# Input normalising on ScalarE and VectorE shared anew, and the low-rank weights' scaling moved to ScalarE, in the first stage of a hybrid encoder

## The chip, the core and the metric
The kernel runs on one core of one Trainium2 chip. The core has a matrix engine (TensorE, PE in the profile; its weight loads are PEld), a vector engine (VectorE, DVE), a scalar engine (ScalarE, ACT), a third elementwise engine (GpSimd, POOL), and a sync engine (SP) that mostly issues DMAs. Each engine takes its own instructions in a fixed order and waits on semaphores for the others. The metric is the time of one launch in microseconds, as the median of several runs.

## The reference
One layer of a post-norm encoder, batch 1, 1024 positions, width 1024, in float32. The input is normalised, projected to 2048 columns, given to four kinds of mixers, projected back, normalised, put through a SwiGLU block and normalised again:

```python
h = _layer_norm(x, ln0_g, ln0_b)
p = h @ w_in[l]
p_ssm, p_rkv, p_conv, p_fft = jnp.split(p, splits, axis=-1)
y_a = _s5_mixer(p_ssm, ...)          # diagonal complex state space, two directions
y_b = _rwkv7_mixer(h, p_rkv, ...)    # delta-rule state update, two directions
y_c = _short_conv_mixer(p_conv, conv_w[l])
y_d = _fourier_mixer(p_fft)
y = jnp.concatenate([y_a, y_b, y_c, y_d], axis=-1)
h = _layer_norm(DEEPNORM_ALPHA * h + y @ w_out[l], ln1_g[l], ln1_b[l])
f = (jax.nn.silu(h @ ffn_w1[l]) * (h @ ffn_w3[l])) @ ffn_w2[l]
h = _layer_norm(DEEPNORM_ALPHA * h + f, ln2_g[l], ln2_b[l])
```

The change touches the first norm and, in the RWKV mixer, the low-rank weights. That mixer blends each position of `h` with its neighbour, channel by channel, before it multiplies by a narrow matrix:

```python
dx = jnp.stack([x_prev, x_next]) - xn
xw = xn + dx * mu_w[:, None, None, :]
xa = xn + dx * mu_a[:, None, None, :]
xg = xn + (0.5 * (x_prev + x_next) - xn) * mu_g
```

Since the blend is linear, the kernel multiplies `h` by `(1 - mu) * w` and by `mu * w`, and adds the second product shifted by one position.

## The kernel before, in words
**Accuracy and tiling.** A float32 matmul is done as three matmuls on rounded parts (`mm3`, L159 to L162): high weights by high input (L160), high weights by low input (L161), low weights by high input (L162). So each operand exists twice: the high part is the value rounded to the matmul's format, the low part is what the rounding left. The input after the norm is kept transposed, channels on the partitions, as `HA` (high) and `HB` (low). The weights of a column block of 128 come in as `wraw`, a cast on ACT gives `wh` (L393), a subtraction on POOL gives `wl` (L394). Blocks 2 and 3 of the first stage go into a larger tile, `wfar`, instead. A column block is 96 matmuls over 256 positions each (four quarters of the positions, eight blocks of channels, three products).

**The norm.** `norm0` goes over eight tiles of 128 positions. Per tile: statistics (`row_stats`, on DVE with a square root on ACT at L183), the normalised tile `xn` (L316, DVE, in place of `xt`), then in two halves of four channel blocks: four transposes on PE into `n0ps` (L322), four evacuations with gain and bias into `hf` (ACT at L332, or DVE at L329), a cast to `HA` (L333, DVE) and a subtraction to `HB` (L334, POOL).

**The stages.** `start` weaves the norm with the first four column blocks, two for S5 and two for the Fourier mixer (384 matmuls). Then `build` weaves two strands. The chain, at high priority, is S5 (its tables `s5w`, then products named `s5tp`, `s5k`, `s5pv`, `s5py`), then the RWKV preparation with the first direction's block inverse (`pre`, `pa` fed by `abd`, `pm` fed by `dmn`), then the scan of 32 steps (`px`, `pt`, `pz`, `po`). The other strand, `beside`, holds the rest of the projection: low-rank weights for two directions and the gate (`lora_project`), the RWKV columns, the convolution, Fourier; and then the second direction's inverse, which the scan needs from its step 17 on, and the first parts of the output projection.

**What sets the order.** The code of both strands is given to a scheduler with priorities; it places instructions on each engine by a modelled time. Both strands are issued only after the three instructions in `norm_end`, one each on DVE, ACT and POOL, so these decide where the norm's work ends on each engine and where the other begins. In the kernel before, DVE's of the three is the last `xn`, so S5's DVE work may start while the norm's casts are still going.

**Low-rank weights.** `weights` in `lora_project` loads a narrow matrix as `lraw`, and L903 multiplies it by `mu` per channel into `lmw` on DVE, eight or sixteen small instructions. `lmw` then goes through cast and subtraction like other weights; POOL subtracts `lmw` from `lraw` (L918, L930, L936), which leaves `(1 - mu) * w`, and that goes through the same. L919 adds the two products into `la`.

## Time and profile before
| | |
|---|---|
| median of 3 runs | 1463.02 us (1460.07 to 1464.85) |
| profiled execution | 1465.01 us |
| its span, first to last instruction | 1462.2 us |
| PE busy | 1323.2 us, 90% |
| DVE busy | 1100.0 us, 75% |
| ACT busy | 621.7 us, 43% |
| POOL busy | 575.7 us, 39% |

The span is 2.8 us shorter than the time of the execution it belongs to; what lies around it no instruction shows. Busy shares are averages over stages of very different kinds, so rows of single stages are needed to say what an engine waits for. A wait is put down to the instruction that released it, with the waiting instruction in front of the arrow.

### The profile page before, as it was taken

What the parts mean: (1) busy time and instruction counts of PE and PEld (TensorE: products, weight loads), DVE (VectorE), ACT (ScalarE), POOL (GpSimd) and SP (SyncE); (2) the same over time, 40 slices, a digit from 0 to 9 for tenths busy, and PEclk for the clock granted to TensorE, in tenths of its full rate; (3) what the DMA queues carried; (4) which work ended last, traced back from release to release, by engine and by line L of the source; (5) the groups of instructions that cost most, each with busy time, mean ns of one, the idle gap of its engine ahead of it and who ended that gap; (6) DMA issues with size and microseconds to landing.
All of it is one profiled execution on the core that took longest, in us unless ns stands there. A gap on an engine that the chain in (4) does not pass through costs nothing.

```text
span 1462.2 us, 23749 instructions
## 1 busy us (share of the span) xinstructions
PE 1323.2 (90%) x9072; PEld 1196.4 (82%) x9072; DVE 1100.0 (75%) x1910; ACT 621.7 (43%) x1205; POOL 575.7 (39%) x524
## 2 busy tenths in 40 slices
PE   6968797977797999999877899999999999999997
PEld 5968787766796787877766899999999999888885
DVE  8997966487997685779999866666676665346888
ACT  4312141656324785761426544444444444332231
POOL 6466663153574332325567633333333331000006
PEclk9989998999899898999999899999999999999999
DMA  6111033122325004244312434444444438996752
GB/s 241 49 54 29 13 94 87 44 70 89 87 73 180 2 15 148 84 128 154 118 70 87 138 123 159 147 147 143 157 147 142 150 137 291 385 315 234 273 188 115
DMA packets 97056, 193.95 MB, mean 133 GB/s; under 512 B 24624, under 2 KB 50864, under 8 KB 96944
## 3 DMA queue, kind: packets, MB, share of 16 engines
q1 hardware_dynamic: 94912, 187.59, 38.3%
q10 hardware_dynamic: 2032, 4.86, 1.0%
q8 instruction: 71, 1.16, 0.3%
q14 instruction: 41, 0.34, 0.1%
HBM read 127.41 MB, written 63.96 MB: 131 GB/s over the span
## 4 chain that ended last, share of the span: by engine, by line
PE 42%; DVE 12%; DMA 3%; issue 2%; ACT 1%; POOL 1%; DVEq 0%; SPq 0%; ACTq 0%; POOLq 0%
PE fx L160 5%; PE fx L162 5%; PE fx L161 5%; PE f L160 4%; PE f L162 4%; PE f L161 4%; PE fy L162 2%; PE fy L160 2%; PE fy L161 2%; DVE acc L1435 1%; PE fz L160 1%; PE fz L161 1%; PE fz L162 1%; DMA fw<-w 1%; PE ops L161 1%
## 5 line engine op out<-in xcount | busy, mean ns | idle before, releaser
L160 PE MATMUL proj<-HA,wh 128*128 128x256 f32 x672 | 195.5, 291 | 14.6 <-DVE la L919 11.8
L160 PE MATMUL fx<-H,fc 128*128 128x256 f32 x704 | 196.9, 284 | 5.7 <-ACT fc L1384 2.2
L161 PE MATMUL proj<-HB,wh 128*128 128x256 f32 x672 | 200.1, 298 | 1.7 <-POOL HB L334 1.7
L162 PE MATMUL proj<-HA,wl 128*128 128x256 f32 x672 | 196.6, 293 | 4.1 <-POOL wl L394 4.1
L162 PE MATMUL fx<-H,fc 128*128 128x256 f32 x704 | 197.8, 282 | 2.6 <-DVE fc L1385 2.6
L1385 POOL TENSOR_TENSOR fc<-fw,fc 128x512 fp32r<-128x512 f32 x96 | 137.3, 1432 | 158.5 <-ACT fc L1384 157.7
L161 PE MATMUL fx<-H,fc 128*128 128x256 f32 x704 | 198.5, 282 | 0.0
L160 PEld LDWEIGHTS proj<-HA,wh 128*128 128x128 f32 x672 | 131.8, 196 | 18.4 <-issue 7.7
L162 PEld LDWEIGHTS proj<-HA,wl 128*128 128x128 f32 x672 | 131.5, 196 | 10.0 <-issue 5.5
L160 PEld LDWEIGHTS fx<-H,fc 128*128 128x128 f32 x704 | 132.5, 190 | 7.8 <-ACT fe L1633 2.7
L161 PEld LDWEIGHTS proj<-HB,wh 128*128 128x128 f32 x672 | 131.5, 196 | 7.0 <-issue 4.8
L162 PEld LDWEIGHTS fx<-H,fc 128*128 128x128 f32 x704 | 133.7, 191 | 2.8 <-DVE fc L1385 2.8
L161 PEld LDWEIGHTS fx<-H,fc 128*128 128x128 f32 x704 | 134.1, 191 | 0.1
L160 PE MATMUL f<-fb,fa 128*128 128x512 f32 x276 | 108.9, 395 | 0.0
L162 PE MATMUL f<-fb,fa 128*128 128x512 f32 x276 | 108.9, 394 | 0.0
L161 PE MATMUL f<-fb,fa 128*128 128x512 f32 x276 | 108.7, 394 | 0.0
L160 PE MATMUL fy<-H,fc 128*128 128x256 f32 x352 | 100.0, 284 | 4.7 <-ACT fe L1642 3.6
L162 PE MATMUL fy<-H,fc 128*128 128x256 f32 x352 | 99.5, 284 | 0.2 <-DVE fc L1385 0.2
L161 PE MATMUL fy<-H,fc 128*128 128x256 f32 x352 | 99.5, 283 | 0.0
L1821 POOL TENSOR_TENSOR acc<-acc,g 128x1024 f32<-128x1024 f32 x4 | 11.6, 2904 | 205.8 <-ACT acc L1820 205.8
L1384 ACT CAST fc<-fw 128x512 fp32r<-128x512 f32 x120 | 73.7, 619 | 31.8 <-POOL fc L1385 15.7
L1385 POOL TENSOR_TENSOR fc<-fs,fc 128x512 fp32r<-128x512 f32 x24 | 33.4, 1391 | 119.4 <-ACT fc L1384 116.0
(602 smaller groups left out, 3761.6 us busy)
## 6 DMA issues: line engine op xcount, KB each, us to landing
fa<-d_f SPq DMA_DIRECT2D x77, 512.0 KB, 3.8
d_f<-fg SPq DMA_DIRECT2D x70, 512.0 KB, 2.9
fw<-w SPq DMA_DIRECT2D x48, 512.0 KB, 3.6
fg<-w SPq DMA_DIRECT2D x44, 256.0 KB, 5.3
wraw<-w_in SPq DMA_DIRECT2D x16, 512.0 KB, 4.0
xt<-x SPq DMA_DIRECT2D x8, 512.0 KB, 8.1
oraw<-w_out SPq DMA_DIRECT2D x8, 512.0 KB, 3.7
yraw<-d_y SPq DMA_DIRECT2D x8, 512.0 KB, 4.1
```

The source lines that it names most:

```text
L160: mm(out, whi, xhi, start=start, stop=False, skip_group_check=shared)
L161: mm(out, whi, xlo, start=False, stop=False, skip_group_check=shared)
L162: mm(out, wlo, xhi, start=False, stop=stop, skip_group_check=shared)
L1384: nc.scalar.copy(out=hi, in_=raw)
L1385: (eng or nc.gpsimd).tensor_tensor(out=lo, in0=raw, in1=hi.bitcast(F32), op=ALU.subtract)
L1435: nc.vector.tensor_tensor(out=ht, in0=ht, in1=self.row4[1], op=ALU.add)
L1821: nc.gpsimd.tensor_tensor(out=o, in0=o, in1=self.g2, op=ALU.mult)
```

## The change
In `norm0`, `xn` is made by an ACT activation (scale `rstd`, bias `nm`), where `nm`, minus the mean times `rstd`, is a new DVE instruction on one column. The first half of the channel blocks is evacuated on ACT and the second on DVE, for all tiles. The cast to `HA` moves from DVE to ACT. The low part `HB` is made by POOL for the first half and by DVE for the second. `norm_end` now holds DVE's last low part, ACT's last cast and POOL's last low part.

In `lora_project`, both products are made by ACT, `mu * w` and, with a new constant `oml`, `(1 - mu) * w`; DVE's L903 and POOL's subtractions go. In the narrowest case the first is written straight into the columns next to the second, so a POOL copy goes as well.

In the first direction's `rk_inverse`, one of the two `abd` copies moves from DVE to ACT.

```diff
--- before.py
+++ after.py
@@ -282,9 +282,15 @@
 
         self.st0 = cp.tile([128, NT, 2], F32, name="st0")
 
+        self.nm0 = cp.tile([128, NT], F32, name="nm0")
+
         self.omu = cp.tile([128, 12], F32, name="omu")
         o, n = VEC["mu_rkv"]
         nc.vector.tensor_scalar(out=self.omu, in0=self.vec[:, o:o + n], scalar1=-1.0, scalar2=1.0,
+                                op0=ALU.mult, op1=ALU.add)
+        self.oml = cp.tile([128, 40], F32, name="oml")
+        o = VEC["mu_w"][0]
+        nc.vector.tensor_scalar(out=self.oml, in0=self.vec[:, o:o + 40], scalar1=-1.0, scalar2=1.0,
                                 op0=ALU.mult, op1=ALU.add)
 
         self.hb0 = cp.tile([128, 8], F32, name="hb0")
@@ -313,8 +319,9 @@
             nc.sync.dma_start(out=xt, in_=A["x"][t * 128:(t + 1) * 128, :])
             mean, rstd = self.row_stats(sp, xt, D, LN_EPS, self.st0[:, t])
             xn = xt
-            xl = nc.vector.tensor_scalar(out=xn, in0=xt, scalar1=mean, scalar2=rstd,
-                                            op0=ALU.subtract, op1=ALU.mult)
+            nm = self.nm0[:, t:t + 1]
+            nc.vector.scalar_tensor_tensor(out=nm, in0=mean, scalar=-1.0, in1=rstd, op0=ALU.mult, op1=ALU.mult)
+            nc.scalar.activation(out=xn, in_=xt, func=AF.Identity, scale=rstd, bias=nm)
             hf = self.t(f"C{1 + t % 2}", [128, 8, 128], "hf")
             for q in range(2):
                 ps = self.ps("q", [128, 4, 128], "n0ps")
@@ -325,13 +332,15 @@
 
                 for k in range(4):
                     g, b = (self.v(x, 4 * q + k) for x in ("ln0_g", "ln0_b"))
-                    if q and t > 1:
-                        nc.vector.tensor_scalar(out=hf[:, 4 * q + k], in0=ps[:, k, :], scalar1=g, scalar2=b,
+                    if q:
+                        xl = nc.vector.tensor_scalar(out=hf[:, 4 * q + k], in0=ps[:, k, :], scalar1=g, scalar2=b,
                                                 op0=ALU.mult, op1=ALU.add)
                     else:
-                        af = nc.scalar.activation(out=hf[:, 4 * q + k], in_=ps[:, k, :], func=AF.Identity, scale=g, bias=b)
-                last = nc.vector.tensor_copy(out=hi, in_=hf[:, r])
-                pl = nc.gpsimd.tensor_tensor(out=self.hlo[:, t, r], in0=hf[:, r], in1=hi.bitcast(F32), op=ALU.subtract)
+                        nc.scalar.activation(out=hf[:, 4 * q + k], in_=ps[:, k, :], func=AF.Identity, scale=g, bias=b)
+                af = nc.scalar.copy(out=hi, in_=hf[:, r])
+                lo = (nc.gpsimd, nc.vector)[q].tensor_tensor(out=self.hlo[:, t, r], in0=hf[:, r], in1=hi.bitcast(F32),
+                                                             op=ALU.subtract)
+                xl, pl = (lo, pl) if q else (None, lo)
             self.norm_end = [xl, af, pl]
             yield 4.5
 
@@ -896,12 +905,16 @@
         def weights(c0, n, mus):
             raw = self.t("P3", [128, NK, 128], "lraw")
             nc.sync.dma_start(out=raw[:, :, :n], in_=A["lora"][:, :, c0:c0 + n])
-            mw = self.t("P2", [128, NK, 128], "lmw")
+            mw = self.t("P2", [128, NK, 128], "lmw") if n > 32 else raw[:, :, n:]
             step = n // len(mus)
-            for k in range(NK):
-                for i, (mu, o) in enumerate(mus):
-                    nc.vector.tensor_scalar_mul(mw[:, k, i * step:(i + 1) * step],
-                                                raw[:, k, i * step:(i + 1) * step], self.v(mu, o + k))
+            base = VEC["mu_w"][0]
+            for own in range(2):
+                for k in range(NK):
+                    for i, (mu, o) in enumerate(mus):
+                        c = slice(i * step, (i + 1) * step)
+                        o2 = VEC[mu][0] + o + k - base
+                        nc.scalar.mul(out=(raw if own else mw)[:, k, c], in_=raw[:, k, c],
+                                      mul=self.oml[:, o2:o2 + 1] if own else self.v(mu, o + k))
             return raw, mw
 
         def padded(tag):
@@ -915,7 +928,6 @@
             la = self.t(f"LA{d}", [128, S], "la")
             lb = padded("P0")
             yield from self.block(self.split(mw), lambda n, ps: nc.scalar.copy(out=lb[:, sl1(n)], in_=ps))
-            nc.gpsimd.tensor_tensor(out=raw, in0=raw, in1=mw, op=ALU.subtract)
             yield from self.block(self.split(raw), lambda n, ps: nc.vector.tensor_tensor(
                 out=la[:, sl(n)], in0=ps, in1=lb[:, 2 * d + n * 512:2 * d + (n + 1) * 512], op=ALU.add))
             nc.scalar.activation(out=la[0:64], in_=la[0:64], func=AF.Tanh)
@@ -927,14 +939,11 @@
         lb = padded("P0")
         yield from self.block(self.split(mw), lambda n, ps: nc.scalar.copy(out=lb[:, sl1(n)], in_=ps))
         nc.vector.tensor_tensor(out=gb, in0=lb[:, 0:S], in1=lb[:, 2:S + 2], op=ALU.add)
-        nc.gpsimd.tensor_tensor(out=raw, in0=raw, in1=mw, op=ALU.subtract)
         yield from self.block(self.split(raw), lambda n, ps: nc.vector.scalar_tensor_tensor(
             out=ga[:, sl(n)], in0=gb[:, sl(n)], scalar=0.5, in1=ps, op0=ALU.mult, op1=ALU.add))
         nc.scalar.activation(out=ga, in_=ga, func=AF.Sigmoid)
         raw, mw = weights(384, 32, (("mu_g", 0),))
         nc.gpsimd.memset(raw[:, :, 64:128], 0.0)
-        nc.gpsimd.tensor_tensor(out=raw[:, :, 0:32], in0=raw[:, :, 0:32], in1=mw[:, :, 0:32], op=ALU.subtract)
-        nc.gpsimd.tensor_copy(out=raw[:, :, 32:64], in_=mw[:, :, 0:32])
         lb = padded("P0")
 
         def evac(n, ps):
@@ -1125,8 +1134,8 @@
             abd = abds[:, n % abds.shape[1]]
             for h in range(2):
                 r = slice(64 * h, 64 * h + 64)
-                eng = nc.gpsimd if d and h else nc.vector
-                eng.tensor_copy(out=abd[r, :, h, :], in_=av[r, p, c:c + 4, 0, :])
+                eng = (nc.gpsimd.tensor_copy if d else nc.scalar.copy) if h else nc.vector.tensor_copy
+                eng(out=abd[r, :, h, :], in_=av[r, p, c:c + 4, 0, :])
             ps = self.ps("pj" if d else ("q", "fs")[n % 2], [128, 4, 2, 64], "pa")
             for e in range(4):
                 nc.tensor.matmul(ps[:, e], bk[:, p, c + e].rearrange("p a t -> p (a t)"),
```

**ACT, the first two tiles.** Before, from the first square root on (`bnr` is the root of the variance, `hf` the evacuated tile, `wh` and `wfar` weight casts):

```order
L183 ACTIVATE bnr_118<-bnmv_116,eps 128x1
L183 ACTIVATE bnr_161<-bnmv_159,eps 128x1
L393 CAST wfar_110<-wraw_107 128x1024
L393 CAST wh_150<-wraw_107 128x1024
L332 ACTIVATE hf_126<-n0ps_127,vec 128x128 x4
L332 ACTIVATE hf_126<-n0ps_138,vec 128x128 x4
L332 ACTIVATE hf_169<-n0ps_170,vec 128x128 x4
L393 CAST wfar_110<-wraw_107 128x1024
L332 ACTIVATE hf_169<-n0ps_181,vec 128x128 x4
L393 CAST wh_193<-wraw_107 128x1024
L183 ACTIVATE bnr_310<-bnmv_308,eps 128x1
```

The same place now; `xt` stands for `xn`, written in place:

```order
L183 ACTIVATE bnr_121<-bnmv_119,eps 128x1
L183 ACTIVATE bnr_165<-bnmv_163,eps 128x1
L402 CAST wfar_113<-wraw_110 128x1024
L324 ACTIVATE xt_114<-xt_114,nm_82,st_81 128x1024
L324 ACTIVATE xt_158<-xt_158,nm_82,st_81 128x1024
L402 CAST wh_154<-wraw_110 128x1024
L339 ACTIVATE hf_130<-n0ps_131,vec 128x128 x4
L402 CAST wfar_113<-wraw_110 128x1024
L339 ACTIVATE hf_174<-n0ps_175,vec 128x128 x4
L340 CAST HA_100<-hf_130 128x512 x2
L402 CAST wh_198<-wraw_110 128x1024
L340 CAST HA_100<-hf_174 128x512 x2
```

Two normalisings and the casts to `HA` have come between the weight casts, and half of the `hf` evacuations have gone.

**POOL, the first low parts.** Before (`HB` is the low part of the input, `wl` and the second rows of `wfar` those of the weights):

```order
L394 TENSOR_TENSOR wfar_110<-wraw_107,wfar_110 128x1024
L394 TENSOR_TENSOR wl_151<-wraw_107,wh_150 128x1024
L334 TENSOR_TENSOR HB_99<-hf_126,HA_97 128x512 x2
L334 TENSOR_TENSOR HB_99<-hf_169,HA_97 128x512
L394 TENSOR_TENSOR wfar_110<-wraw_107,wfar_110 128x1024
L334 TENSOR_TENSOR HB_99<-hf_169,HA_97 128x512
L394 TENSOR_TENSOR wl_194<-wraw_107,wh_193 128x1024
```

And now:

```order
L403 TENSOR_TENSOR wfar_113<-wraw_110,wfar_113 128x1024
L403 TENSOR_TENSOR wl_155<-wraw_110,wh_154 128x1024
L403 TENSOR_TENSOR wfar_113<-wraw_110,wfar_113 128x1024
L341 TENSOR_TENSOR HB_102<-hf_130,HA_100 128x512
L403 TENSOR_TENSOR wl_199<-wraw_110,wh_198 128x1024
L341 TENSOR_TENSOR HB_102<-hf_174,HA_100 128x512
```

Three of the weights' low parts stand ahead of the first `HB`, and a fourth ahead of the second tile's; before it were two and three.

**DVE, the end of the norm.** Before, the first S5 instructions (from L528 on) stood ahead of the norm's last evacuations and casts:

```order
L333 CAST HA_98<-hf_710 128x512
L575 TENSOR_TENSOR s5x_93_924<-vec,s5x_93_924 128x16
L578 TENSOR_TENSOR s5x_93_924<-vec,s5x_93_924 128x16
L528 TENSOR_SCALAR xr_947<-s5x_93_924 128x16
L529 TENSOR_SCALAR xk_946<-xr_947 128x16
L579 TENSOR_SCALAR s5x_93_924<-s5x_93_924 128x16
L530 TENSOR_SCALAR xk_946<-xk_946 128x16
L329 TENSOR_SCALAR hf_710<-n0ps_722,vec 128x128 x4
L531 SCALAR_TENSOR_TENSOR xr_947<-xk_946,xr_947 128x16
L580 TENSOR_SCALAR s5x_93_924<-s5x_93_924 128x16
L333 CAST HA_98<-hf_710 128x512
L532 SCALAR_TENSOR_TENSOR xr_947<-xk_946,xr_947 128x16
```

Now, where L341 is a low part of the input and L537 the line that was L528:

```order
L341 TENSOR_TENSOR HB_103<-hf_537,HA_101 128x512
L341 TENSOR_TENSOR HB_103<-hf_682,HA_101 128x512
L336 TENSOR_SCALAR hf_721<-n0ps_733,vec 128x128 x4
L341 TENSOR_TENSOR HB_103<-hf_721,HA_101 128x512
L537 TENSOR_SCALAR xr_953<-vec 128x16
L663 TENSOR_SCALAR s5x_93_951<-vec 128x16
L538 TENSOR_SCALAR xk_952<-xr_953 128x16
L539 TENSOR_SCALAR xk_952<-xk_952 128x16
L540 SCALAR_TENSOR_TENSOR xr_953<-xk_952,xr_953 128x16
```

S5's work on DVE begins behind the norm's last low part.

## Rows read from the trace of the kernel before
**Rows 1.** The windows; span, length, then busy us and instructions of PE, PEld, DVE, ACT, POOL; PEclk, DMA share, GB/s:
```profile
18.80:74.10 55.30, 53.81 (x431) 53.20 (x431) 54.91 (x215) 18.35 (x41) 29.87 (x36) 1.00 0.23 79
74.10:172.80 98.70, 73.38 (x545) 71.30 (x545) 88.23 (x171) 17.24 (x26) 66.99 (x53) 0.86 0.12 29
```

**Rows 2.** Waits of PE, 0 to 172 us: waited for, us, times, longest:
```profile
PE proj L160 <- DVE la L919: 11.8, 2, 6.9
...
PE s5tp L705 <- DVE s5w L513: 8.2, 1, 8.2
PE proj L162 <- POOL wl L394: 3.2, 1, 3.2
```

**Rows 3.** Waits of PE, 172 to 480 us:
```profile
PE pa L1132 <- DVE abd L1129: 10.7, 3, 4.5
...
PE s5py L825 <- DVE s5x L814: 8.3, 2, 7.0
PE pm L1211 <- ACT dmn L1218: 5.8, 1, 5.8
PE pm L1211 <- DVE dmn L1193: 2.5, 1, 2.5
```

**Rows 4.** DVE by line and shape, 0 to 260 us: count, busy us, mean ns, idle before:
```profile
L316 DVE TENSOR_SCALAR xt<-xt,st 128x1024 f32<-128x1024 f32 x8 | 10.4, 1325 | 0.0
...
L333 DVE CAST HA<-hf 128x512 fp32r<-128x512 f32 x16 | 9.3, 590 | 1.6 <-ACT hf L332 1.6
L903 DVE TENSOR_SCALAR lmw<-lraw,vec 128x64 f32<-128x64 f32 x32 | 9.1, 355 | 0.0
L329 DVE TENSOR_SCALAR hf<-n0ps,vec 128x128 f32<-128x128 f32 x24 | 8.2, 400 | 0.0
...
L919 DVE TENSOR_TENSOR la<-proj,lb 128x512 f32<-128x512 f32 x4 | 2.7, 677 | 0.0
```

**Rows 5.** DVE in order of time: start, us, line, operation:
```profile
59.45 0.42 DVE L333 CAST HA<-hf 128x512 fp32r<-128x512 f32 x1
...
97.86 1.87 DVE L903 TENSOR_SCALAR lmw<-lraw,vec 128x64 f32<-128x64 f32 x11
...
99.98 0.68 DVE L513 TENSOR_TENSOR s5w<-s5x 128x512 f32<-128x512 f32 x1
```

**Rows 6.** ACT by line and shape, 0 to 260 us:
```profile
L332 ACT ACTIVATE hf<-n0ps,vec 128x128 f32<-128x128 f32 x40 | 14.7, 474 | 7.1 <-PE n0ps L322 5.1 <-POOL HB L334 2.0
L393 ACT CAST wh<-wraw 128x1024 fp32r<-128x1024 f32 x5 | 5.3, 1063 | 13.5 <-PE proj L161 7.9 <-POOL abd L1123 4.3 <-DMA wraw<-w_in 1.3
```

**Rows 7.** PE in order of time, with the wait ahead of a row in brackets:
```profile
18.83 0.58 PE L161 MATMUL proj<-HB,wh 128*128 128x256 f32 x1 [1.35 <-POOL HB L334]
...
92.10 0.28 PE L161 MATMUL proj<-HB,wh 128*128 128x256 f32 x1
92.22 0.28 PE L162 MATMUL proj<-HA,wl 128*128 128x256 f32 x1
100.71 0.69 PE L705 MATMUL s5tp<-ident,s5w 128*128 128x128 f32 x2 [8.22 <-DVE s5w L513]
```

**Rows 8.** POOL in order of time, the first row of the start:
```profile
9.26 2.37 POOL L394 TENSOR_TENSOR wfar<-wraw,wfar 128x1024 fp32r<-128x1024 f32 x1 [7.88 <-ACT wfar L393]
```

**Rows 9.** POOL by line and shape, 0 to 260 us:
```profile
L334 POOL TENSOR_TENSOR HB<-hf,HA 128x512 fp32r<-128x512 f32 x16 | 22.1, 1395 | 19.5 <-DVE HA L333 9.1 <-DVE xk L529 6.9 <-DVE xr L532 2.3
L394 POOL TENSOR_TENSOR wl<-wraw,wh 128x1024 fp32r<-128x1024 f32 x5 | 14.6, 2915 | 7.1 <-PE proj L162 6.9
```

**Rows 10.** POOL and DVE in order of time, the same stretch:
```profile
77.16 2.38 POOL L394 TENSOR_TENSOR wl<-lraw,wh 128x1024 fp32r<-128x1024 f32 x1
...
77.18 2.40 DVE L516 TENSOR_TENSOR s5x<-s5qr,s5qi 128x16 f32<-128x16 f32 x1
```

**Rows 11.** PE in order of time, the same matmuls in two steps of the scan:
```profile
514.16 1.06 PE L1306 MATMUL po<-ring,ring 128*128 128x128 f32 x8
...
518.47 1.06 PE L1306 MATMUL po<-ring,ring 128*128 128x128 f32 x8
```

## The prediction
> **What bounds the kernel now.** I read the windows first, then TensorE's waits, then the lines of each engine, and at last single stretches of the timeline. PE is 90% busy over the span, so only its idle time and its slow stretches can be won. The change touches the first 172.8 us and a few places behind. From 18.8 to 74.1 us PE is busy 53.8 of 55.3 us: nothing to win there but the moment at which it begins. DVE is full there too (54.9). From 74.1 to 172.8 us PE is busy only 73.4 of 98.7 us, DVE 88.2, ACT 17.2, and the granted clock is 0.86, so a part of that stretch ran at 1.2 instead of 2.4 GHz [rows 1]. PE idles because DVE is late: 11.8 us in two waits for `la`, 8.2 us for `s5w` (the tables of S5), and 3.2 us for `wl` from POOL [rows 2]. After 172.8 us it waits again for what the S5 and RWKV chain hands on: `abd` 10.7, `s5x` 8.3, `dmn` 5.8 and 2.5 us [rows 3]. So that chain sets the pace, and the projection's matmuls are the filler that PE does meanwhile. The change takes work off DVE ahead of the chain.
>
> **The change, part by part.** *DVE in the norm.* It loses L316 (8 instructions, 10.4 us) and the 16 casts L333 (9.3 us). It gains 8 low parts of 128x512 (nearest row: L919, a two-input DVE operation of that size, 0.68 us; 5.4 us), 8 more emptied 128x128 blocks, four each for tiles 0 and 1, at 0.40 us (3.2 us), and 8 negated means of 128x1, which no row shows: between nothing and those 0.40, I take 0.2 us as the smaller size should be nearer the fixed part (1.6 us) [rows 4]. Net relief: 9.5 us. *DVE in the low-rank weights.* All of L903 goes; its largest kind alone is 32 instructions and 9.1 us busy [rows 4]. Sixteen of them stood in the norm and sixteen around the S5 tables, eleven directly ahead of the `s5w` for which PE waits [rows 5] and five behind it.
>
> *The S5 tables.* DVE is full up to the first `s5w`, which began at 99.98 and ended at 100.66 us [rows 5], so what is taken away ahead of it moves it: 9.5 us and 27 of the 32 L903 at 9.1/32 = 0.28 us, 7.7 us; together 17.2, which gives 83.5 us. But S5's DVE instructions, which stood among those of the norm (whose last cast ran at 59.45 us [rows 5]), now stand behind all of the norm's, and the norm goes at ACT's pace. ACT per tile: `xn` 1.15 us (the 128x1024 cast takes 1.06 [rows 6]), four `hf` at 14.7/40 = 0.37 us [rows 6], two casts of 128x512 at half of 1.06, and a small square root that I put at 0.2: 3.9 us, 31 us for eight tiles; four weight casts 4.2 and four evacuations of 128x512, 2.1: 37 us, from about 8 us on (the first cast of `wfar` frees POOL at 9.26 [rows 8]), so 46 us if ACT never waits. It does wait for PE's transposes, and I take 51 us for the norm's end, with 46 and 60 as its bounds. The first `s5w` then comes at about 87 us.
>
> *ACT's low-rank muls.* 64 of 128x64, 16 of 128x128 and 16 of 128x32 stand in place of 48 muls on DVE and four subtractions on POOL. No row shows ACT at 128x64: from above the 0.474 us of a 128x128 alone, from below half of the 0.37 at which those follow each other, 0.19 [rows 6]. I take 0.27, nearer to the rows in a sequence: 32 a direction, 8.7 us (6 to 15.2). They lie beside idle ACT time (81 of 98.7 us [rows 1]), and cost nothing if the second direction's are done when the copies of S5's transposes, behind them in ACT's order, are wanted.
>
> A 128x128 block with two pointers costs 0.37 us on ACT and 8.2/24 = 0.34 us on DVE [rows 4, 6]; here the two engines are alike. The Trainium skill, "ScalarE: Activation LUTs", Rules for kernel authors, says to use VectorE and not ScalarE for multiplies and adds, DVE being up to about three times faster per element in bf16. At that full factor a mul would take 0.85 us by the L903 row and a direction 27 us, and the S5 copies would be held back by 27 − 8.7 = 18 us: slower than before; the two fp32 rows speak against it.
>
> *The start.* On POOL the first tiles' low parts now stand behind a second `wfar` and a `wl`. From 9.26 us [rows 8]: `wfar` 2.4, 0.4 of waiting for the cast of `wh` (ACT makes both `xn` first), `wl` 2.9, `wfar` 2.4, HB of tile 0 1.4, `wl` 2.9, HB of tile 1 1.4 [rows 8, 9]: 23.0 us. PE waited for the low part until 18.83 [rows 7]: +4.2 us. Where `wl` takes only the 2.4 us of a `wfar` and HB is shorter in the same measure, +2.9; with two more waits for ACT, +6. All of the first 384 matmuls move by it.
>
> DVE and POOL disturb each other: a DVE operation on 128x16 took 2.40 us beside a POOL one of 2.38 us and ended with it [rows 10]. So a low part on DVE may cost as much as the POOL operation beside it. The Trainium skill, "SBUF — State Buffer", SBUF: two separate sides, says that a DVE operation with two SBUF inputs and a GpSimd operation hold one port pair in turn, each for its whole instruction; the trace agrees. By that rule the two low parts of a tile never run side by side, and if each of the 8 on DVE waits for half a POOL operation, 0.7 us by the HB row, DVE's relief in the norm falls from 9.5 to 4 us.
>
> *The sum,* in PE time, from the profiled execution of 1465.0 us (span 1462.2 and 2.8 around it). Start: +4.2. `wl`: −3.2, as POOL has no subtraction for these weights ahead of it. `s5w`: 8.2 to about 1, −7 [rows 2]. First `la`, 11.8 − 6.9 = 4.9 [rows 2], to about 1, −4, since its evacuation stands behind the tables now and they are early. Second `la`, 6.9: I expect other waits of about 4 there, for S5's own steps, −3. Clock: 0.86 on 98.7 us means 28 us at 1.2 GHz [rows 1], much of it idle; with shorter waits −2 (0 to −6). Displaced matmuls: counted in the order, 492 of the projection stood ahead of the first `s5tp` and 463 now, 2201 ahead of the first `pm` and 2106 now. These 95 at 0.117 us (92.10 to 92.22 [rows 7]), 11.1 us, are done later; they fill the waits at `pm`, 5.8 and 2.5 [rows 3], and 2.8 is left over: +2.8. `abd` half on ACT: −2 of the 10.7 [rows 3] (0 to −4). The second inverse now follows the 14th step of the scan instead of the 12th; a step is 518.47 − 514.16 = 4.3 us [rows 11], so 0 to +8.6, and as the order has its successors back in place by step 22, +2. Together 4.2 − 3.2 − 7 − 4 − 3 − 2 + 2.8 − 2 + 2 = −12.2 us: 1452.8 in terms of the profiled execution, which is 2.0 above the median; as a median 1451.
>
> **The rivals.** *D: the chain keeps its whole lead.* PE's idle time from 74.1 to 172.8 us, 25.3 us [rows 1], goes entirely, and so do 4 us of slow clock, less 4.2 at the start: −25, 1438. For it: DVE loses 17 us ahead of the tables and more behind. Against it: PE's order holds fewer projections ahead of each step of the chain, so the chain is asked sooner.
> *B: the waits only move.* As 29 to 95 fewer matmuls stand ahead of each step, 3 to 11 us of the chain's lead is used up by that, and the wait of `s5w` comes back at S5's later products and at `abd`: 4.2 − 3.2 − 7 + 5 = −1, 1462 (1458 to 1466). For it: those steps were late before as well [rows 3]. Against it: DVE's L903 and the subtractions are gone there too.
> *C, slower: ACT sets the pace.* `xn`, `hf` and the casts of a tile follow each other on ACT, and the muls stand ahead of the S5 copies. If the norm ends after 58 to 60 us, the tables come no earlier than when they stood among the norm's work, and from there it decides. Price: start +4.2, copies held back +5 (muls at 0.474 us, 15.2 a direction), `la` 0, `wl` −3.2, `s5w` −2, displaced matmuls +2.8, `abd` −2, two scan steps +8.6, and −4 of waits that the displaced matmuls fill: +9, 1472. For it: ACT waits for PE between its parts of a tile. Against it: ACT was busy 18.4 of 55.3 us [rows 1].
>
> **How the numbers follow.** Forecast 0.55, its own range 1444 to 1458; D 0.13; B 0.16; C 0.16. About 0.3%, 4.4 us, is what a measurement of this kernel can tell from no change: faster is below 1458.6, slower above 1467.4. Faster: 0.55, 0.13 and 0.01 of B, 0.69; same: the rest of B, 0.15; slower: 0.16. The range 1438 to 1468 takes in the forecast, B, the upper half of D and C's mildest part.
>
> **What would show it.** In the profile after: the first L161 at 23 us; the norm's last DVE instruction at about 51; the first `s5tp` at 86 to 93 us with about 1 us of waiting; no wait for `la` over 2 us; no wait at `pm`; a granted clock above 0.86 from 78 to 170 us. The forecast is wrong if the norm ends after 58 us, if the wait for `s5w` stays near 8, or if a new wait of over 6 us stands at an S5 product or at `abd`.

## The result, and the profile after

The changed kernel takes 1472.72 us (median of 4 runs, 1470.34 to 1473.76), against 1462.41 us for the kernel before beside it (4 runs, 1460.07 to 1464.85): a ratio of 1.0065 with a 95% interval of 1.0046 to 1.0084, so about 10 us slower where I forecast 12 us faster. The profiled execution took 1472.97 us, with a span of 1471.3. Two of the kernels below have one execution far longer than their others (1514.90 us in hold_pool, 1827.31 in hold_lo2), which is in their medians but not in their ratios.

First the windows of the changed kernel: start and length of the stretch, then busy us and instructions of PE, PEld, DVE, ACT and POOL, granted clock, share and rate of the DMAs. The stretches are the rest of the norm's stage, the next 94.6 us (these answer to [rows 1]), and then the whole span cut at five events: the first transposes of the scan (464.7), the products `pc` of the scan's step 24 (624.9), those of its last step, 31 (675.0), and the first `fx` of the FFN (777.1).

```profile
22.83:78.20 55.37, 54.26 (x437) 54.05 (x438) 45.69 (x236) 38.65 (x89) 18.18 (x29) 1.00 0.16 53
78.20:172.80 94.60, 75.66 (x581) 74.14 (x581) 81.46 (x105) 33.47 (x91) 61.34 (x48) 0.87 0.14 34
0.00:464.70 464.70, 383.37 (x2750) 351.01 (x2751) 340.75 (x628) 214.11 (x384) 219.52 (x222) 0.93 0.26 84
464.70:624.90 160.20, 147.66 (x1063) 123.31 (x1061) 119.16 (x336) 112.34 (x316) 58.35 (x113) 0.98 0.22 71
624.90:675.00 50.10, 45.32 (x269) 38.08 (x267) 43.67 (x102) 21.50 (x56) 16.98 (x16) 0.93 0.57 179
675.00:777.10 102.10, 80.97 (x363) 65.33 (x363) 89.60 (x130) 29.15 (x51) 51.18 (x27) 0.90 0.24 79
777.10:1471.30 694.20, 665.90 (x4634) 621.05 (x4632) 470.09 (x663) 286.86 (x520) 205.93 (x135) 0.98 0.52 182
```

The kernel before, cut at the same five events:

```profile
0.00:469.30 469.30, 386.71 (x2785) 354.00 (x2786) 377.69 (x685) 174.99 (x270) 245.99 (x238) 0.93 0.28 86
469.30:633.20 163.90, 150.35 (x1025) 124.78 (x1024) 117.79 (x342) 110.09 (x314) 52.80 (x110) 0.93 0.17 56
633.20:675.40 42.20, 38.76 (x252) 33.43 (x251) 37.69 (x88) 20.21 (x51) 16.42 (x15) 0.96 0.66 203
675.40:774.70 99.30, 85.01 (x376) 67.03 (x375) 94.16 (x135) 28.47 (x50) 55.82 (x29) 0.95 0.26 86
774.70:1462.20 687.50, 662.35 (x4642) 617.14 (x4640) 472.63 (x663) 287.99 (x522) 204.67 (x135) 0.98 0.54 185
```

Read event by event, the changed kernel is 4.6 us ahead when the scan begins and 8.3 us ahead at step 24. Then it takes 50.1 us for the last seven steps where it took 42.2, and the lead is 0.4. The out-projection takes 102.1 us in place of 99.3, and the FFN to the end 694.2 in place of 687.5. So the front did become shorter, and all of the loss lies in stages of which the change does not touch an instruction. Each of these times comes from one execution, though: after_pin below, whose instructions stand in the changed kernel's order up to 733 us, began its scan 2.3 us and reached step 24 3.3 us later than the changed kernel, so differences of 3 us between two profiles carry little weight.

The front first. DVE, full before, is now busy 45.7 of 55.4 us in the norm's stage. What PE waited for up to 172 us (us in total, times, longest), to be read against [rows 2]:

```profile
...
PE proj L160 <- DVE la L931: 8.4, 1, 8.4
PE s5tp L714 <- DVE s5w L522: 5.3, 1, 5.3
PE s5k L752 <- DVE s5x L740: 5.2, 1, 5.2
PE proj L161 <- POOL HB L341: 4.2, 2, 3.1
```

And from 172 to 480 us, against [rows 3]:

```profile
PE pre L1095 <- DVE prep L1087: 10.5, 3, 6.8
PE pa L1141 <- DVE abd L1138: 8.3, 2, 6.8
PE gps L965 <- ACT lg L957: 6.1, 1, 6.1
PE s5py L834 <- DVE s5x L823: 5.5, 1, 5.5
...
PE pm L1220 <- ACT dmn L1225: 1.9, 1, 1.9
...
PE pm L1220 <- DVE dmn L1202: 1.0, 1, 1.0
```

The waits have become other waits. That for `wl` is gone, as forecast; those for `dmn` fell from 8.3 to 2.9 us, where I had forecast none; but `s5w` is still waited for 5.3 us, `la` 8.4, and new ones stand at the S5 products (`s5x`, 5.2) and at the gate (`lg`, 6.1). By the windows PE idled 82.6 of 469.3 us before the scan, and 81.3 of 464.7 us now: 1.3 us less. The other 3.3 us of the lead are 35 matmuls fewer ahead of the scan (2750 for 2785), which it does in the scan's stretch.

PE's first product with a low part (its start, then its duration, and in brackets the wait before it), against [rows 7]:

```profile
22.83 0.58 PE L161 MATMUL proj<-HB,wh 128*128 128x256 f32 x1 [3.09 <-POOL HB L341]
```

The first S5 transpose, in the same columns:

```profile
92.12 1.12 PE L714 MATMUL s5tp<-ident,s5w 128*128 128x128 f32 x4 [5.29 <-DVE s5w L522]
```

They came at 22.83 (forecast 23.0) and 92.12 us (forecast 86 to 93, with a wait of about 1; it was 5.3). The end of the norm on DVE and the first S5 instruction, against [rows 5]:

```profile
52.48 1.36 DVE L341 TENSOR_TENSOR HB<-hf,HA 128x512 fp32r<-128x512 f32 x1 [0.82 <-ACT HA L340]
53.76 0.51 DVE L537 TENSOR_SCALAR xr<-vec 128x16 f32<-128x16 f32 x1
```

The norm ended at 53.8 us (forecast 51, bounds 46 to 60). And what single operations took, on DVE and on ACT (mean ns behind the busy us), against [rows 4, 6]:

```profile
L341 DVE TENSOR_TENSOR HB<-hf,HA 128x512 fp32r<-128x512 f32 x8 | 9.4, 1173 | 8.7 <-ACT HA L340 8.7
```

And the same of ACT:

```profile
L339 ACT ACTIVATE hf<-n0ps,vec 128x128 f32<-128x128 f32 x32 | 12.2, 460 | 1.5 <-DVE HB L341 1.0 <-POOL HB L341 0.5
L324 ACT ACTIVATE xt<-xt,nm,st 128x1024 f32<-128x1024 f32 x8 | 9.6, 1238 | 1.3 <-DVE nm L323 1.3
...
L916 ACT ACTIVATE lraw<-lraw,oml 128x64 f32<-128x64 f32 x32 | 8.2, 338 | 0.0
L916 ACT ACTIVATE lmw<-lraw,vec 128x64 f32<-128x64 f32 x32 | 8.0, 335 | 6.2 <-DMA lraw<-lora 6.2
```

ACT's muls of 128x64 cost 8.2/32 = 0.26 us each in a row (forecast 0.27). A low part on DVE cost 1.17 us in the mean, where the nearest row had been 0.68.

### The profile page after: what moved, and what is told of

It is laid out like the page before. It is cut to its first block, busy times and chain, and to the rows that moved or that the text cites. A ratio compares the mean times of both kernels' runs of the same rounds, so it can differ in the third digit from the quotient of the medians.

```text
span 1471.3 us, 23815 instructions
## 1 busy us (share of the span) xinstructions
PE 1323.2 (90%) x9072; PEld 1198.8 (81%) x9072; DVE 1063.3 (72%) x1855; ACT 664.0 (45%) x1325; POOL 552.0 (38%) x511
## 4 chain that ended last, share of the span: by engine, by line
PE 46%; DVE 19%; ACT 4%; DMA 4%; issue 3%; POOL 0%; SPq 0%; DVEq 0%; ACTq 0%; POOLq 0%
PE fx L160 5%; PE fx L162 4%; PE fx L161 4%; PE f L160 4%; PE f L162 4%; PE f L161 4%; PE fy L160 2%; PE fy L161 2%; PE fy L162 2%; DMA fw<-w 2%; PE pc L1326 1%; PE fz L160 1%; PE fz L161 1%; PE fz L162 1%; DVE tpr L1183 1%
## 5 line engine op out<-in xcount | busy, mean ns | idle before, releaser
L160 PE MATMUL proj<-HA,wh 128*128 128x256 f32 x672 | 198.8, 296 | 12.1 <-DVE la L931 8.4
L161 PE MATMUL proj<-HB,wh 128*128 128x256 f32 x672 | 198.8, 296 | 4.2 <-POOL HB L341 4.2
L162 PE MATMUL proj<-HA,wl 128*128 128x256 f32 x672 | 200.3, 298 | 0.0
L161 PE MATMUL fx<-H,fc 128*128 128x256 f32 x704 | 200.0, 284 | 0.0
L160 PEld LDWEIGHTS fx<-H,fc 128*128 128x128 f32 x704 | 134.0, 192 | 10.2 <-ACT fc L1393 4.2
L162 PEld LDWEIGHTS fx<-H,fc 128*128 128x128 f32 x704 | 135.4, 192 | 5.1 <-DVE fc L1394 3.1
L161 PEld LDWEIGHTS proj<-HB,wh 128*128 128x128 f32 x672 | 131.6, 196 | 9.0 <-POOL HB L341 4.7
L161 PEld LDWEIGHTS fx<-H,fc 128*128 128x128 f32 x704 | 135.2, 192 | 0.1
L161 PE MATMUL f<-fb,fa 128*128 128x512 f32 x276 | 108.7, 394 | 0.0
L161 PE MATMUL fy<-H,fc 128*128 128x256 f32 x352 | 100.2, 285 | 0.0
```

Of the source, the lines that this page charges most:

```text
L160: mm(out, whi, xhi, start=start, stop=False, skip_group_check=shared)
L161: mm(out, whi, xlo, start=False, stop=False, skip_group_check=shared)
L162: mm(out, wlo, xhi, start=False, stop=stop, skip_group_check=shared)
```

## The experiments

One thing was found before the first of them, by comparing orders: how the instructions stand from the first out-projection matmul on is not a matter of degree. The norm's part alone, the low-rank weights' part alone and both together give, on PE, DVE, ACT and POOL, instruction for instruction the order of the changed kernel there (I call it the late order). Each of the two with the `abd` copies gives an order that is nearly that of the kernel before (the early one). The parts could so be tried with either. In the profiles the two orders differ alike in every kernel of this set: with the late one (changed kernel, norm_only, lora_only, after_pin, no_abd) the last seven steps of the scan took 47.4 to 50.2 us and the out-projection 102.0 to 104.0, with the early one (before, norm_abd, lora_abd, start) 41.7 to 44.5 and 98.0 to 99.3.

**The norm's part, with and without the `abd` copies.** The edit of norm_only is the diff's hunks in `norm0` and the tile `nm0`, and nothing else; norm_abd adds:

```diff
-                eng = nc.gpsimd if d and h else nc.vector
-                eng.tensor_copy(out=abd[r, :, h, :], in_=av[r, p, c:c + 4, 0, :])
+                eng = (nc.gpsimd.tensor_copy if d else nc.scalar.copy) if h else nc.vector.tensor_copy
+                eng(out=abd[r, :, h, :], in_=av[r, p, c:c + 4, 0, :])
```

Expected of norm_only:

> The norm's part of the change alone: low-rank weights and abd copies as before. From the first out-projection matmul on, its instructions stand in exactly the order of the changed kernel, on PE, DVE, ACT and POOL. Theory A (the order of the out-projection and what follows costs some 10 us or more, the front is a gain): slower than before all the same, 1464 to 1472 us, with a wait of PE for acc of 8 us or more ahead of a transpose ot near the end of the out-projection. Theory B (the front's lead is lost because the out-projection is limited by DVE and POOL work that starts at a fixed time, whatever its order): 1462 to 1466, no such wait of more than 5 us beyond what before has (6.7 us for H).

Measured: 1481.91 us, ratio 1.0132 (1.0116 to 1.0148). Slower even than Theory A's range. Expected of norm_abd:

> The norm's part and the abd copies, low-rank weights as before. From the first out-projection matmul on the order on PE is that of before but for a few rows. Theory A: the lead of the front stays in the total: 1454 to 1460 us, and 8 us or more faster than norm_only, which has nearly the same front. Theory B: within 4 us of norm_only.

Measured: 1469.24 us, ratio 1.0046 (1.0029 to 1.0062): 12.7 us faster than norm_only. At the scan's step 24 the two stand within 2.7 us of each other, and norm_abd is the later one (638.4 for 635.7 us); from there to the end norm_only took 847.0 us and norm_abd 829.9. Theory A holds in the difference. It fails in the sum: the norm's part is no gain even with the early order, and norm_abd began its scan 4.8 us later than before.

**The low-rank weights' part, with and without the `abd` copies.** The edit of lora_only is the diff's hunks in `lora_project` and the constant `oml`. Expected:

> The low-rank weights' part alone: norm and abd copies as before; PE starts at 18.8 us. From the first out-projection matmul on exactly the order of the changed kernel. Theory A: 1464 to 1473 us with the long wait for acc, although nothing in the norm is changed. Theory B: 1456 to 1463, as its start is not later. Theory C (the norm's part on ACT is what costs, by itself): faster than before, 1452 to 1460.

Measured: 1488.87 us, ratio 1.0173 (1.0157 to 1.0189). Expected of lora_abd:

> The low-rank weights' part and the abd copies, norm as before; out-projection in nearly the order of before. Theory A: 1452 to 1460 us, 8 us or more faster than lora_only. Theory B: within 4 us of lora_only. Theory C: the same as lora_only, faster than before.

Measured: 1469.08 us, ratio 1.0036 (1.0020 to 1.0053): 19.8 us faster than lora_only, from the same norm and the same weights. In the profiles 9.3 us of the difference lie ahead of step 24, where the `abd` copies count, and 12.4 behind it, where the order does. Theories B and C fall: lora_only is the slowest kernel of all, with no later start and nothing of the norm moved to ACT. Neither part alone is faster than before, which Theory A had said they would be with the early order. For lora_abd the traces show where the time went: its scan began 8.1 us earlier than before, but needed 172.4 us to step 24 for 163.9, with the late gate that hold_mix shows below.

**PE's transposes pinned.** The most visible wait of the late order is one of PE at the end of the out-projection, where transposes of tile 3 (`ot`) stand ahead of the matmuls of the last tiles; the lines are PE's of the changed kernel:

```profile
746.43 1.94 PE L1527 MATMUL ot<-ident,acc 128*128 128x128 f32 x8 [12.19 <-DVE acc L1475]
751.91 0.80 PE L160 MATMUL ops<-owa,y 128*128 128x512 f32 x1 [3.54 <-DVE acc L1464]
```

The longest wait of that stage in the kernel before:

```profile
748.65 0.77 PE L160 MATMUL ops<-owa,y 128*128 128x512 f32 x1 [6.75 <-ACT H L1384]
```

The edit, in `turn` (the matmuls' handles are kept in `ops_mm` by `out_product`):

```diff
-                for k in range(4):
-                    kt = 4 * q + k
-                    nc.tensor.transpose(ps[:, k, :], ht[:, kt * 128:(kt + 1) * 128], self.ident)
+                at = self.ops_mm[(1, 0) if q == 0 and t == 3 else (0, 1)].ins if j == 2 else None
+                with self.tc.issue_after(at) if j == 2 else nullcontext():
+                    for k in range(4):
+                        kt = 4 * q + k
+                        nc.tensor.transpose(ps[:, k, :], ht[:, kt * 128:(kt + 1) * 128], self.ident)
```

> The changed kernel with its instructions unchanged; only the transposes ot of the third turn (tiles 3 and 2) are queued on PE behind the out-projection's matmuls of tile 1, first half (the first four) and of tile 0 (the rest), which is where the kernel before has them. Theory A (the order of the out-projection's end costs some 10 us and the FFN's begin some 5 more): 1456 to 1463 us; the 12.2 us wait of PE for acc before ot, and most of the waits at the FFN's begin, are gone; all before the 288th out-projection matmul as in the changed kernel. Theory B (DVE and POOL limit that stage, whatever PE's order): within 4 us of the changed kernel's 1472.7.

Measured: 1471.1 us, ratio 1.0056 (1.0040 to 1.0073). Theory A in this form was wrong, and the number is Theory B's. The wait only moved to the matmul behind:

```profile
756.44 0.76 PE L160 MATMUL ops<-owa,y 128*128 128x512 f32 x1 [17.79 <-DVE acc L1466]
```

The bank that this matmul wants is emptied by a DVE addition (L1466), and PE went on only behind it. That DVE's order puts other work ahead of this addition is likely, but was not tried. So the cost doesn't sit in those transposes alone; PE's order at one place is not the order of the stage.

**The first two tiles as before.** Here tiles 0 and 1 keep `xn`, the casts, the evacuations and the low parts of the kernel before, so that the start is not later:

```diff
-            nc.scalar.activation(out=xn, in_=xt, func=AF.Identity, scale=rstd, bias=nm)
+            if t < 2:
+                nc.vector.tensor_scalar(out=xn, in0=xt, scalar1=mean, scalar2=rstd, op0=ALU.subtract, op1=ALU.mult)
+            else:
+                nc.scalar.activation(out=xn, in_=xt, func=AF.Identity, scale=rstd, bias=nm)
...
-                    if q:
+                    if q and t > 1:
...
-                af = nc.scalar.copy(out=hi, in_=hf[:, r])
-                lo = (nc.gpsimd, nc.vector)[q].tensor_tensor(out=self.hlo[:, t, r], in0=hf[:, r], in1=hi.bitcast(F32),
+                af = (nc.vector.tensor_copy if t < 2 else nc.scalar.copy)(out=hi, in_=hf[:, r])
+                lo = (nc.gpsimd, nc.vector)[q and t > 1].tensor_tensor(out=self.hlo[:, t, r], in0=hf[:, r], in1=hi.bitcast(F32),
```

> The change without its part in the first two tiles: those two have xn and the casts on DVE, all evacuations on ACT and all low parts on POOL, as before; tiles 2 to 7, the low-rank weights and the abd copies as in the changed kernel. The out-projection and the FFN then stand in nearly the order of before. Theory A: the lead of about 8 us that the changed kernel had at its 288th out-projection matmul, the 4 us of the later start, and no loss behind: 1449 to 1456 us. If the front's lead were lost in the scan and the out-projection whatever the order (Theory B): 1460 to 1466.

Measured: 1466.17 us (six runs, 1463.13 to 1469.10), ratio 1.0024 (1.0009 to 1.0038): 6.6 us faster than the changed kernel and not what Theory A said; by the number alone it stands next to Theory B, 0.2 us above its range. Its first L161 came at 19.02 us, 3.8 us earlier than in the changed kernel, and its first `s5tp` at 92.6, 0.5 us later than there. So the 3.8 us did not reach the chain; PE used them for 33 more matmuls ahead of `s5tp`. From step 24 to the first `fx` it took 143.8 us (before 141.5, changed kernel 152.2): with the early order most of that loss is gone. Why the whole is 3 us slower than before is not shown; the profiled execution, 1463.13 us, was the fastest of the six.

**The `abd` copies undone**, the changed kernel otherwise:

> The changed kernel with both abd copies of the first direction on DVE, as before; its order from the first out-projection matmul on is exactly the changed kernel's. If the half of the abd copies on ACT is worth what I put it at (2 us, at most 4): 1473 to 1477 us. Theory D (the copies on ACT delay what ACT does for the chain): 1468 to 1471.

Measured: 1480.10 us, ratio 1.0118 (1.0096 to 1.0140), with the same order from the out-projection on. Half of the `abd` copies on ACT is worth 7.4 us here in the medians and 4.8 in the profiled executions, against the 2, at most 4, that I had put it at. In its trace the last projection matmul ran at 476.1 us for 468.6, and the last `pm`, of the second inverse, at 575.3 for 567.6.

**The scan's end held.** What the late order does at the end of the scan is seen on PE in the changed kernel; `ops` are out-projection matmuls of the first tile, `px` and `pc` products of the scan:

```profile
647.01 0.39 PE L1306 MATMUL pz<-ring,HB1f 128*128 128x128 f32 x2
647.16 0.47 PE L162 MATMUL ops<-owa,y7l 128*128 128x512 f32 x1
...
651.45 0.39 PE L162 MATMUL ops<-owa,y7l 128*128 128x512 f32 x1
651.68 0.27 PE L1382 MATMUL pgn<-ident,yacc 128*128 128x128 f32 x1
651.88 0.44 PE L1293 MATMUL px<-ring,ak 128*64 128x128 f32 x4
...
652.82 0.36 PE L1326 MATMUL pc<-ring,ring 128*128 128x96 f32 x2
```

From 647.16 to 651.88 us there are nineteen `ops`, 0.23 us apart, and behind them the scan's next `px`. They are filler by their purpose, but their place in PE's order is fixed, and a step of the scan stands behind them. The kernel before has no `ops` there; its first runs at 654.88 us. The edit lets the scan's steps go first (`pc_at[n]` is the last `pc` of step n):

```diff
-        yield from self.until(("rk_out", 4))
+        yield from self.until(("rk_out", 1))
...
-                self.mm3(ps, hi[:, k, :], lo[:, k, :], self.wo8[k][0][:, sl],
-                         self.wo8[k][1][:, sl], i == 0, i == 7)
+                m = 3 * (8 * n + i)
+                at = self.pc_at[28 if m < 13 else 29 if m < 35 else 30].ins if t == 7 else None
+                with self.tc.issue_after(at) if at else nullcontext():
+                    self.mm3(ps, hi[:, k, :], lo[:, k, :], self.wo8[k][0][:, sl],
+                             self.wo8[k][1][:, sl], i == 0, i == 7)
```

> The changed kernel with the first out-projection tile's work traced later and its matmuls queued on PE behind the products pc of the scan's steps 28 (the first 13), 29 (the next 22) and 30 (the rest); everything up to that place stands as in the changed kernel, and what follows falls into nearly the order of before. Theory A2 (the order from the scan's last steps on costs: in the five kernels with that order the last six steps took 45 to 46 us where they took 36 in the four others, the out-projection 3 to 5 us more, the FFN some 5 more): 1455 to 1462 us, with pc of step 25 to step 31 in 36 to 38 us. Theory B (the front's lead is lost there whatever the order): 1469 to 1474.

Measured: 1458.07 us (eight runs, 1456.21 to 1460.25), ratio 0.9966 (0.9955 to 0.9977). That is 14.7 us faster than the changed kernel, by an edit that changes PE's order only from 643 us on, and 5 us faster than before. The scan's end in it, where the `px` and the `pc` come first:

```profile
647.75 0.43 PE L1293 MATMUL px<-ring,ak 128*64 128x128 f32 x2 [0.92 <-ACT ring L1282]
648.11 0.46 PE L1326 MATMUL pc<-ring,ring 128*128 128x96 f32 x2
...
649.56 0.48 PE L160 MATMUL ops<-owa,y7h 128*128 128x512 f32 x1
```

And its windows, cut at the same events as above:

```profile
0.00:464.90 464.90, 383.62 (x2750) 351.24 (x2751) 341.11 (x628) 214.19 (x384) 219.68 (x222) 0.93 0.26 84
464.90:625.30 160.40, 147.85 (x1064) 123.41 (x1062) 119.42 (x336) 112.39 (x316) 58.35 (x113) 0.98 0.22 70
625.30:669.20 43.90, 39.82 (x247) 34.32 (x246) 38.64 (x98) 21.32 (x55) 14.42 (x14) 0.92 0.61 193
669.20:765.90 96.70, 84.78 (x377) 67.06 (x376) 92.19 (x134) 28.37 (x50) 55.21 (x28) 0.96 0.26 85
765.90:1456.20 690.30, 666.71 (x4643) 621.63 (x4641) 471.92 (x663) 288.51 (x522) 206.38 (x135) 0.98 0.53 184
```

In its first two rows the stretches are as long as the changed kernel's to within 0.2 us. Then the last seven steps take 43.9 us for 50.1, the out-projection 96.7 for 102.1, the rest 690.3 for 694.2: 6.2 + 5.4 + 3.9 = 15.5 us. Theory A2 is shown in the time, and Theory B fallen: the lead was there and was lost to the order. One sign of A2 was missed: from step 25 to step 31 it took 39.2 us and not 36 to 38 (45.9 in the changed kernel, 36.3 before; the figures that A2 starts from, 45 to 46 and 36, are 43.1 to 46.0 and 35.8 to 37.3 in the profiles). Of the three parts the last, 3.9 us, is not clear of what single profiles differ by: after_pin took 690.7 there.

**The same edit in the kernel before**, as a control:

> The kernel before with the same edit as in hold and nothing of the change. Its scan end is then in nearly the order of before, but the end of its out-projection falls into that of the changed kernel (transposes of tile 3 ahead of the last two tiles' matmuls). Theory A2: 6 to 10 us slower than before, 1469 to 1473, though not one instruction is changed: what the out-projection and the FFN's begin lose. Theory B: as before, 1460 to 1466.

Measured: 1473.79 us, ratio 1.0073 (1.0055 to 1.0091), 0.8 us above Theory A2's range. Without one instruction of the change, a kernel 10.7 us slower. Its last seven steps took 39.8 us, less than before; its out-projection took 109.1, with waits like those of the changed kernel:

```profile
747.28 1.94 PE L1523 MATMUL ot<-ident,acc 128*128 128x128 f32 x8 [10.18 <-DVE acc L1471]
752.76 0.79 PE L160 MATMUL ops<-owa,y 128*128 128x512 f32 x1 [3.54 <-DVE acc L1460]
```

**Low parts, with the scan's end held.** hold_pool gives POOL all of them again; DVE's instruction in `norm_end` is then the last evacuation, so S5 need not wait there for a low part:

```diff
-                lo = (nc.gpsimd, nc.vector)[q].tensor_tensor(out=self.hlo[:, t, r], in0=hf[:, r], in1=hi.bitcast(F32),
+                lo = nc.gpsimd.tensor_tensor(out=self.hlo[:, t, r], in0=hf[:, r], in1=hi.bitcast(F32),
```

> As hold, with all low parts of the transposed input on POOL as before (none on DVE). Theory E (the two engines take turns there, so dividing gains nothing): within 3 us of hold. Theory F (dividing shortens the norm): the norm ends 4 us later or more, and the time is 3 to 8 us over hold.

Measured: 1455.39 us, ratio 0.9947 (0.9930 to 0.9964). It is 2.7 us under hold, and the two intervals overlap; in the profiles it is ahead by 4.0 us at the scan's start (460.9 for 464.9) and keeps 3.6 to the end. Theory F is refuted, in its sign too: the last low part ended at 51.8 us, in hold at 53.9, and DVE came to S5 at 48.1 us for 53.8. Dividing the low parts gains nothing, as Theory E said; that it costs is likely (the eight runs of hold lie between 1456.21 and 1460.25, three of hold_pool's four between 1454.37 and 1455.80), but not clear of the intervals. It is the fastest kernel of this study.

hold_lo2 gives DVE both low parts of the first two tiles:

```diff
-                lo = (nc.gpsimd, nc.vector)[q].tensor_tensor(out=self.hlo[:, t, r], in0=hf[:, r], in1=hi.bitcast(F32),
+                lo = (nc.gpsimd, nc.vector)[1 if t < 2 else q].tensor_tensor(out=self.hlo[:, t, r], in0=hf[:, r], in1=hi.bitcast(F32),
```

> As hold, with both low parts of the first two tiles on DVE, so that PE's first L161 doesn't wait behind POOL's four low parts of weights: first L161 at 19.5 to 21 us in place of 22.8. If the start moves all that follows: 2 to 3 us faster than hold. If the later waits on the chain take it up: within 1 us of hold.

Measured: 1459.81 us, ratio 0.9970 (0.9957 to 0.9982). Its first L161 came at 21.06 us, 1.8 earlier, and no gain can be measured: as in start, the first `s5tp` is no earlier for it (92.2 for 92.4 us in hold).

hold_mix is hold_pool with the first tile's low parts on DVE:

```diff
-                lo = nc.gpsimd.tensor_tensor(out=self.hlo[:, t, r], in0=hf[:, r], in1=hi.bitcast(F32),
+                lo = (nc.vector if t < 1 else nc.gpsimd).tensor_tensor(out=self.hlo[:, t, r], in0=hf[:, r], in1=hi.bitcast(F32),
```

> As hold_pool, with both low parts of the first tile alone on DVE, so that PE's start waits for one low part less on POOL: first L161 at about 21.5 us in place of 23.05; the order from the scan's end on is that of hold. If the start's lateness reaches the end: 1452.5 to 1454.5 us, 1 to 2 us under hold_pool's 1455.4. If the waits on the chain (s5w, la, s5x) take it up: 1454.5 to 1457.

Measured: 1468.22 us, ratio 1.0035 (1.0022 to 1.0049): 12.8 us slower than hold_pool for two instructions on another engine, and both of my cases missed. Its first L161 came at 22.09 us. Its order from the out-projection on is, against the expectation, not exactly that of hold, but nothing is lost there: from step 24 to the end it took 830.4 us and hold_pool 831.4. The largest wait of PE between 172 and 480 us names the place (total us, times, longest); in hold_mix:

```profile
PE gps L966 <- ACT lg L958: 18.4, 1, 18.4
```

The same row of hold_pool:

```profile
PE gps L966 <- ACT lg L958: 6.4, 1, 6.4
```

In hold_mix the RWKV gate's sigmoid comes 17.9 us later (233.1 for 215.2), the last projection matmul runs at 484.2 us for 464.8, and the last `pm` of the second inverse, whose code stands behind the projection's, at 576.1 for 563.8; step 24 of the scan is reached 16.5 us later, though the scan began only 0.4 later. What stands ahead of the sigmoid shows on DVE, where the gate's addition `lg` comes behind four scan instructions of S5 (`TENSOR_TENSOR_SCAN`, not the RWKV scan); in hold_mix the first of the four and the addition behind them:

```profile
213.81 4.47 DVE L803 TENSOR_TENSOR_SCAN s5xw<-s5tt,s5x 64x1024 f32<-64x1024 f32 x1
...
225.25 2.10 DVE L954 TENSOR_TENSOR lg<-lb 32x1024 f32<-32x1024 f32 x1
```

In hold_pool the addition runs ahead of them, the first of which begins at 215.29:

```profile
209.14 2.81 DVE L954 TENSOR_TENSOR lg<-lb 32x1024 f32<-32x1024 f32 x1
```

lora_only and lora_abd have the same wait (18.7 and 18.8 us) and the same late end of the projection (486.3 and 484.0). So there is a second place at which the order falls one way or the other. No edit of that place alone was tried.

## Why the prediction was wrong, point by point

**The step that failed** is the sum itself, in its last term, "and as the order has its successors back in place by step 22, +2". With it I closed the ledger at the second inverse, and put all that follows at nothing, as if it stood as before. It did not. From step 24 to the end the changed kernel took 846.4 us of its span where before took 829.0; hold, with the same front to within 0.4 us at step 24, took 830.9, and 14.7 us less in the medians. The order that I had for the prediction showed this, had I read it to its end: twenty-five `ops` stand ahead of the products `pc` of the scan's step 28 in it, and none in the kernel before. A second step failed beside it, the size of the front.

**The front's terms.** Forecast −12.2 us in the total; hold, in which only 1.9 us are lost behind step 24, measured −5.0. The start was sized rightly (+4.0 for +4.2) but did not belong in the chain's sum: start and hold_lo2 begin earlier and are at `s5tp` no earlier, and hold_lo2 gained nothing measurable at the end. `wl`, −3.2: right. `s5w`: −2.9 in place of −7, as DVE's first `s5w` began at 91.4 us and not at 87, and PE came to it with 29 matmuls fewer done and waited at 86.8 us already. `la`: the first wait is gone, −4.9 for −4; the second grew from 6.9 to 8.4 in place of −3, and a new wait of 5.2 for `s5x` stands ahead of it, at 112.9 us. The gate's 6.1 us was in no term. `dmn`: 8.3 to 2.9, where the displaced matmuls were to fill it all. The `abd` copies: the wait went from 10.7 to 8.3 us, near the −2 (0 to −4); taken out of the changed kernel, in no_abd, they were worth 7.4, an error in the change's favour. The clock: 0.87 on 94.6 us for 0.86 on 98.7, by the prediction's working 24.6 us at 1.2 GHz for 28; what that was worth no run shows.

**The rivals.** B, "the waits only move", was right for the front up to the scan: PE's idle time shrank by 1.3 us of 82.6. Its range, 1458 to 1466, was missed, as it put the later order at nothing too; hold, without that loss, lies at its lower end. C gave the right time, 1472, by luck: it decided at a norm's end of 58 to 60 us, and the norm ended at 53.8; ACT's muls cost 0.26 us, near the value that I chose. D fell with the front.

**The two rules weighed.** That two engines take turns held. Six of the eight low parts on DVE began while POOL was at an instruction and ended 0.55 us behind it, after 0.84 to 1.54 us; the two that found POOL idle took 0.69. One of each, the first ending at 53.84 us behind POOL's 53.28 (its own line stands above, at 52.48), the second alone:

```profile
52.00 1.28 POOL L341 TENSOR_TENSOR HB<-hf,HA 128x512 fp32r<-128x512 f32 x1 [2.16 <-ACT HA L340]
```

```profile
47.99 0.69 DVE L341 TENSOR_TENSOR HB<-hf,HA 128x512 fp32r<-128x512 f32 x1 [0.48 <-ACT HA L340]
```

So the eight low parts took DVE 9.4 us and not the 5.4 of the ledger. The Trainium skill, "SBUF — State Buffer", SBUF: two separate sides, says of such a pair that the loser waits for the whole instruction; the trace agrees. How much of the 2.7 us between hold and hold_pool is due to this is not shown, as the end of the norm on DVE moved with it.

ACT's mul of 128x64 took 0.26 us where DVE's took 0.28. The Trainium skill's rule for multiplies, "ScalarE: Activation LUTs", Rules for kernel authors, is to use VectorE, and a mul at the full factor that it states for bf16 was estimated at 0.85 us; these fp32 tiles don't show it.

**What stays open.** Why the last stage differs by 3.9 us between the changed kernel and hold (694.2 for 690.3) is not settled, since the FFN's order differs as well and single profiles differ by as much; nor which of the engines' orders makes the out-projection slow, of which after_pin shows only that it is not PE's transposes alone; nor what makes the gate's addition fall behind S5's scan instructions on DVE in some kernels.

## What to carry to other kernels

Where a scheduler orders the whole program from modelled times, a change at the front can move what stands 600 us later, as it did here, and by whole blocks: compare the orders to the end of the program before adding up a front, and hold that order fixed when a part is to be measured. Low-priority filler in an in-order queue is no longer filler: it has a fixed place, and the step of the chain behind it waits. And a gain ahead of a chain counts only as far as the engine that waits is released at the next step too: add up idle time over all of the chain, not wait by wait.

## What the runs showed that I had not expected

Two instructions of about a microsecond on another engine made 12.8 us (hold_mix against hold_pool), and an edit without any changed arithmetic made 10.7 us slower (before_hold) or 14.7 faster (hold). Moving eight of the first direction's sixteen `abd` copies from DVE to ACT was worth 7.4 us in the medians, more than the 5.0 of the whole change in hold. And an earlier start of PE by 1.8 us (hold_lo2) was worth nothing that could be measured.
